# Hybrid RWKV7 and Fox block on one core: group norm split from the chain, inverse transfers on ScalarE's queue, outputs in bursts of four chunks, three gates moved

## The chip, the cores and the metric

The kernel runs on one core of a Trainium2 chip. The metric is the time of one execution on the device in microseconds (us); three runs of the kernel before are shown. The engines are PE (TensorE), DVE (VectorE), ACT (ScalarE), POOL (GpSimd) and SP (SyncE, which here only issues transfers). Each engine works through its own instructions in a fixed order.

## The reference

One block on x of 1024 tokens by 1024 features, float32, one layer:

```python
h = _rmsnorm(x, norm_g)
u_a, u_b, u_g = split(h @ w_in)
y_a = _rwkv7_mixer(u_a, ...) @ w_out_a     # token shift, 8 heads of 64, recurrent state, group norm, silu gate
y_b = _fox_mixer(u_b, ...) @ w_out_b       # 8 heads of 64, causal softmax with forget gates, silu gate
g_a, g_b = split(u_g, 2)
merged = sigmoid(g_a) * y_a + sigmoid(g_b) * y_b
x = x + merged @ w_out
return _rmsnorm(x, final_norm_g)
```

The mixer of RWKV7 is a scan over tokens, state = state*w + (state a) b + v k, y = state r. After it comes a normalisation of each head's 64 values (mean, variance, the norm of groups), then a bonus and the gate.

## The kernel before

Features lie on partitions, tokens on the free axis. x is normed, transposed, and kept as a high and a low part (hTH, hTL); every projection is three passes of matmuls (L311 to L313: high by high, high by low part of x, low part of the weight by high), which PE takes 512 columns at a time. A weight tile is loaded by SP (L218), its high part is cast on ACT (L203), and its low part is subtracted on POOL (L206).

The scan is done in chunks of 64 tokens. There are four **units**, (p, n): p is a group of four heads, n a half of the sequence, in the order (0,0), (0,1), (1,0), (1,1), called units 0 to 3 here. Each has two functions:

- **prep** (from L471): decays, scores within chunks (psc, L565, masked by DVE into QL and Q, L569), then for the 32 triangles of 32 by 32 per head pair an inverse by substitution on DVE. For it the blocks go from QL to a DRAM tile ld by four DMAs (L598), back by one into lt (L602), with one triangle per partition; 30 steps of two DVE operations (L639 etmp, L643) invert them in place; then td (L645, one DMA) and eight DMAs into Tb (L649) bring them back. DVE transposes them into TW (L655), and PE and ACT make the off-diagonal blocks: pw (L661), TW (L663), pz (L669), Tb (L671). Beside the inverse PE makes pk (L628).
- **chain** (from L680): eight chunks in a row, each px (L694), pu (L709), po (L719) on PE with DVE and ACT between, and every four chunks the output matmuls py (L734, 16 per four chunks) and an addition to yv. Behind the eight chunks the same function holds the group norm (L746 to L772): DVE, transposes pt on PE (L761), a gate, and a DMA to yab.

All else before attention is **bulk**, which fills PE while a unit waits: projections of the second group of heads, the 24 gate tiles (ps_gg: 48 matmuls of 512 columns each, in two halves of 24; ACT takes each half out of PSUM at L376, or L334 and DVE for some, and a DMA of ACT's queue stores it as gab<-gt, L359), and the projections of attention (pf, L907 to L909, 24 matmuls of 256 columns each, taken out by ACT as xn<-pf, L910, and squared, L912; pfv, the values). Until attention the bulk has two PSUM banks (tag pj).

Then **attention** for p = 0 to 3 (two heads each): norm_qk transposes the normed q and k (pqk, pqq, L941), writes KA and QA; QA's high part is copied by DMA to the other 64 partitions (L959, L960); attend makes scores (sc, L994), softmax, transposes (pt, L1018) and outputs (L1038, L1039). Beside it run the projections of the next p and the gates that are left. At the end **merge**: pma and pmb (w_out_a, w_out_b, with ya and yb, whose memory is that of hTL and a pool of its own), and the output projection pz.

What sets the order: a scheduler of the framework places the instructions of all engines from their priorities, which follow the program's text, shifted by `order(offset)`. A bulk stretch has an offset of LATER (1000000), a chain one of -LATER. How many gates lie where is written in three tables, by unit (RFILL) and by attention p (FPRE ahead of, FFILL behind the next projection):

```python
RFILL = [5, 6, 6, 2]
FPRE = [1, 1, 2, 0]
FFILL = [1, 3, 2, 0]
```

The first four numbers take 19 gates; the five that are left go to p = 0 (two) and p = 1 (three), and none is left for p = 2 and 3. `tc.issue_after(ins)` makes the instructions inside it stand behind ins.

Of the kernel before, what the change touches and what calls it, by code (L numbers as in the profile page):

```python
# [9 lines left out]
F32 = mybir.dt.float32  # L10
# [61 lines left out]
T1B = 3  # L72
RFILL = [5, 6, 6, 2]
FPRE = [1, 1, 2, 0]
FFILL = [1, 3, 2, 0]

# [14 lines left out]
def kernel(  # L91
# [30 lines left out]
    @contextmanager  # L122
    def order(offset):

        tc.cur_priority += offset
        yield
        tc.cur_priority -= offset
# [350 lines left out]
    def prep(pp_, n):  # L478
# [117 lines left out]
        for e, _, *qs in half:  # L596
            for i, q in enumerate(qs):
                nc.sync.dma_start(  # L598
                    ld[e, i].transpose([1, 0, 2]),
                    QL[q, e].rearrange("p h c t -> p (h c) t")[:, :, HB * i : HB * i + HB],  # L600
                )
        nc.sync.dma_start(lt3, ld.rearrange("e i g s t -> (e i g) s t"))  # L602

# [40 lines left out]
        td = dp.tile([2, 2, NG, HB, HB], F32, tag="td", name=f"td{u}")  # L644
        nc.sync.dma_start(td.rearrange("e i g s t -> (e i g) s t"), lt3)  # L645
        for e, _, *qs in half:
            for i, q in enumerate(qs):
                for h in range(2):
                    nc.sync.dma_start(  # L649
                        Tg[q, h, :, q], td[e, i, UC * h : UC * h + UC].transpose([1, 0, 2])  # L650
                    )
# [26 lines left out]
    def chain(pp_, n, d):  # L678
# [4 lines left out]
        for c in range(UC):  # L683
# [24 lines left out]
            for h in range(2):  # L708
                nc.tensor.matmul(pu[:, h * C : (h + 1) * C], Tb[:, c, h, :], xs[:, h * C : (h + 1) * C], start=True, stop=True)  # L709
            for e, own, other in pairs:  # L710
# [5 lines left out]
            if gc < NCH - 1:  # L716
                po = pp.tile([P, HALF], F32, tag="xus", name=f"po{u}_{c}")
                for e, own, other in pairs:
                    nc.tensor.matmul(po[:, e * P : (e + 1) * P], BKt[:, e, c, :], SV[:, e, c, :], start=True, stop=True)  # L719
                for e, own, other in pairs:  # L720
# [8 lines left out]
            if c % 4 == 3:  # L729
                py = pp.tile([P, HALF], F32, tag="y", name=f"py{u}_{c}").rearrange("p (c h i) -> p c h i", h=2, i=C)  # L730
                for c_ in range(c - 3, c + 1):
                    for h in range(2):
                        for e, own, other in pairs:
                            nc.tensor.matmul(  # L734
                                py[own, c_ % 4, h, :], Q[:, e, h, c_, :], SV[:, e, c_, h * C : (h + 1) * C],
                                start=True, stop=True,
                            )
                yc = yv[:, c - 3 : c + 1]
                nc.vector.tensor_add(yc, yc, py)


        G = 2 * UC
        st = rp.tile([P, 4, G], F32, tag="st", name=f"stat{u}")
# [180 lines left out]
    def norm_qk(p, xn, rr):  # L924
# [10 lines left out]
        for n in range(2):  # L935
            xg = xn[n].rearrange("p b (g i) -> p (b g) i", i=HD)
            (nc.gpsimd if n in NORMPOOL else nc.vector).tensor_mul(xg, xg, rr[n].unsqueeze(2).broadcast_to([P, 16, HD]))
            for c, key in ((1, "k"), (0, "q")):
# [16 lines left out]
                if key == "q":  # L955
                    nc.sync.dma_start(qlo[:, HS[n]], ql.bitcast(F32))
            if n == 1:
                QAf = QA.bitcast(F32)
                nc.sync.dma_start(QAf[B, 0, :], QAf[A, 0, :])  # L959
                nc.sync.dma_start(QAf[A, 1, :], QAf[B, 1, :])  # L960
        return KA, QA, qlo, cb
# [156 lines left out]
    for i, (p, n) in enumerate(units):  # L1118
        d = prep(p, n)
        if i + 1 == len(units):  # L1120
            open_early()
        with bulky():
            if i == 0:
                proj_rkv(2)
                proj_rkv(3)
            fill(RFILL[i], 0)
            if i + 1 == len(units):
                qk = project_qk(0)
                project_v(0)
                forget()  # L1130
        with order(-LATER):
            chain(p, n, d)
    open_late()
# [96 lines left out]
```

## Time and profile before

| | us |
|---|---|
| three runs | 1168.89, 1172.01, 1174.45 (median 1172.01) |
| the profiled execution | 1171.96 |
| its span, first to last instruction | 1170.3 |
| PE busy | 1064.0 (91%) |
| DVE busy | 725.5 (62%) |
| ACT busy | 459.7 (39%) |
| POOL busy | 284.8 (24%) |

The span is cut by the trace into: norm and transposes until about 50 us, first projections until 130, unit 0 until 243, unit 1 until 382, unit 2 until 511, unit 3 until 640, the last group norm until 677, attention from about 692 to 1000, merge until 1076, output projection until the end. Busy times of a PE whose matmuls overlap are modelled; how fast it goes is read from the distance between the starts of two neighbours. The granted clock is 1.00 at 2.4 GHz and 0.50 at 1.2 GHz.

### The profile page before, as it was taken

The numbers are of one execution on the slowest core, as the hardware profiler recorded it, in microseconds if no ns is written. First come the engines' busy times: TensorE is split into PE (matmuls) and PEld (weight loads), VectorE is DVE, ScalarE is ACT, GpSimd is POOL, SyncE is SP. The second block draws the span as 40 slices with busy tenths as digits, with TensorE's granted clock in tenths as the row PEclk, the third lists the DMA queues.
The fourth block names the chain that finished last, engine by engine and source line by source line (L and its number), as shares of the span: only waits on it lengthen the run. The fifth ranks groups of instructions, "written<-read, shape, count | busy, mean of one in ns | idle before, by whom it ended". The sixth has DMA issues, their size and how long they took to land. (4 is left out here: it accounts for less than half of the span.)

```text
span 1170.3 us, 18157 instructions
## 1 busy us (share of the span) xinstructions
PE 1064.0 (91%) x6591; PEld 873.6 (75%) x6591; DVE 725.5 (62%) x1855; ACT 459.7 (39%) x969; POOL 284.8 (24%) x296
## 2 busy tenths in 40 slices
PE   3897998999989898999989979999989788999997
PEld 3676775867768776777888878887968766877886
DVE  7514676588745866386847449686377577466145
ACT  5534232434224331443233346554355355232222
POOL 4420320125110341114201222313222211251400
PEclk9998999999999998999999989999999899999999
DMA  6156434124341343213311151423142150663223
GB/s 207 48 158 211 131 81 114 55 90 123 101 113 46 119 118 108 64 55 83 92 28 38 41 177 42 122 59 91 36 140 86 43 165 19 203 205 114 95 91 126
DMA packets 126043, 118.20 MB, mean 101 GB/s; under 512 B 33361, under 2 KB 91842, under 8 KB 125954
## 3 DMA queue, kind: packets, MB, share of 16 engines
q1 hardware_dynamic: 113664, 94.99, 27.8%
q10 hardware_dynamic: 11714, 21.52, 5.0%
q8 instruction: 52, 0.85, 0.3%
q0 software_dynamic: 576, 0.54, 0.2%
q14 instruction: 37, 0.30, 0.1%
HBM read 79.23 MB, written 35.68 MB: 98 GB/s over the span
## 5 line engine op out<-in xcount | busy, mean ns | idle before, releaser
L311 PE MATMUL ps_gg<-hTH,wH_gg 128*128 128x512 f32 x384 | 158.5, 413 | 3.3 <-DVE gt L338 2.2
L313 PE MATMUL ps_gg<-hTH,wL_gg 128*128 128x512 f32 x384 | 159.4, 415 | 0.0
L312 PE MATMUL ps_gg<-hTL,wH_gg 128*128 128x512 f32 x384 | 157.9, 411 | 0.0
L206 POOL TENSOR_TENSOR wL_gg<-w_gg,wH_gg 128x1024 fp32r<-128x1024 f32 x24 | 60.2, 2508 | 269.6 <-ACT wH_gg L203 263.2
L311 PEld LDWEIGHTS ps_gg<-hTH,wH_gg 128*128 128x128 f32 x384 | 73.4, 191 | 19.3 <-DVE gt L338 3.0
L313 PEld LDWEIGHTS ps_gg<-hTH,wL_gg 128*128 128x128 f32 x384 | 73.9, 192 | 14.6
L312 PEld LDWEIGHTS ps_gg<-hTL,wH_gg 128*128 128x128 f32 x384 | 73.5, 191 | 13.5
L907 PE MATMUL pf<-wqkH,hTH 128*128 128x256 f32 x256 | 74.7, 292 | 0.0
L908 PE MATMUL pf<-wqkL,hTH 128*128 128x256 f32 x256 | 74.7, 292 | 0.0
L909 PE MATMUL pf<-wqkH,hTL 128*128 128x256 f32 x256 | 74.7, 292 | 0.0
L376 ACT ACTIVATE gt<-ps_gg 128x512 f32<-128x512 f32 x40 | 23.9, 598 | 99.9 <-PE ps_gg L313 89.3
L1005 ACT ACTIVATE pr<-pr,mm 128x128 f32<-128x128 f32 (+3 forms) x64 | 49.9, 780 | 28.3 <-DVE mm L1001 27.4
L639 DVE TENSOR_TENSOR etmp<-lt 64x30 f32<-64x30 f32 (+14 forms) x120 | 51.4, 429 | 10.9 <-issue 7.3
L1183 PE MATMUL pz<-wo,mH 128*128 128x512 f32 (+1 forms) x136 | 53.1, 390 | 2.9 <-ACT mH L1092 2.9
L706 ACT ACTIVATE ws<-state,WC 64x64 f32<-64x64 f32 x112 | 38.7, 345 | 40.2 <-DVE state L726 33.5
L1185 PE MATMUL pz<-wo,mL 128*128 128x512 f32 (+1 forms) x136 | 52.6, 387 | 0.0
L1018 PE MATMUL pt<-ident,pr 128*128 128x128 f32 x288 | 48.2, 275 | 4.4 <-DVE pr L1009 4.4
L1184 PE MATMUL pz<-wo,mH 128*128 128x512 f32 (+1 forms) x136 | 52.2, 384 | 0.0
L908 PEld LDWEIGHTS pf<-wqkL,hTH 128*128 128x128 f32 x256 | 49.9, 195 | 0.5
L907 PEld LDWEIGHTS pf<-wqkH,hTH 128*128 128x128 f32 x256 | 49.9, 195 | 0.2
L909 PEld LDWEIGHTS pf<-wqkH,hTL 128*128 128x128 f32 x256 | 49.9, 195 | 0.2
L643 DVE TENSOR_TENSOR lt<-lt,etmp 64x30 f32<-64x30 f32 (+14 forms) x120 | 46.7, 390 | 3.8
(333 smaller groups left out, 2829.5 us busy)
## 6 DMA issues: line engine op xcount, KB each, us to landing
w_gg<-in_w_in_dram SPq DMA_DIRECT2D x24, 512.0 KB, 3.7
gab<-gt ACTq DMA_DIRECT2D x48, 256.0 KB, 2.1
xt<-in_x_dram SPq DMA_DIRECT2D x8, 512.0 KB, 5.8
wqk<-in_w_in_dram SPq DMA_DIRECT2D x16, 256.0 KB, 3.3
cb<-cumd SPq DMA_DIRECT2D x8, 512.0 KB, 5.4
yt<-yab SPq DMA_DIRECT2D x16, 256.0 KB, 3.4
ta<-gab SPq DMA_DIRECT2D x16, 256.0 KB, 3.5
wot<-in_w_out_dram SPq DMA_DIRECT2D x16, 256.0 KB, 2.9
```

The costliest lines, as they stand in the source:

```text
L206: nc.gpsimd.tensor_sub(wL[:, k], w[:, k], wH[:, k])
L311: nc.tensor.matmul(ps, wH[:, k, :], rH[:, k, ts_], start=(k == 0), stop=False)
L312: nc.tensor.matmul(ps, wH[:, k, :], rL[:, k, ts_], start=False, stop=False)
L313: nc.tensor.matmul(ps, wL[:, k, :], rH[:, k, ts_], start=False, stop=(k == nk - 1))
L639: nc.vector.tensor_mul(tm, lt3[:, s, s + 1 :].unsqueeze(1).broadcast_to([4 * NG, s, m]), lt3[:, :s, s].unsqueeze(2).broadcast_to([4 * NG, ...
L907: nc.tensor.matmul(ps, hTH[:, k, bs], wH[:, kk, :], start=(k == 0), stop=False)
L908: nc.tensor.matmul(ps, hTH[:, k, bs], wL[:, kk, :], start=False, stop=False)
L909: nc.tensor.matmul(ps, hTL[:, k, bs], wH[:, kk, :], start=False, stop=(k == KD - 1))
L1005: nc.scalar.activation(pr[:, :w], pr[:, :w], AF.Exp, bias=last, scale=-1.0, accum_out=mm[:, 2:3])
L1183: nc.tensor.matmul(ps, mH[:, k, bs], oH[:, k, c], start=(k == 0), stop=False)
L1184: nc.tensor.matmul(ps, mH[:, k, bs], oL[:, k, c], start=False, stop=False)
L1185: nc.tensor.matmul(ps, mL[:, k, bs], oH[:, k, c], start=False, stop=(k == KD - 1))
```

## The change

It has five parts. RFILL, FPRE and FFILL take 16 gates before attention instead of 19 and leave eight: one for p = 0, two for p = 1, three for p = 2, two for p = 3. The 14 DMAs of each unit's inverse (ld, lt, td, Tb) are issued by ACT instead of SP. The py matmuls stand behind the last po of their four chunks. The group norm is a function of its own, norm_out, with a priority behind the next unit's preparation, save for the last unit. QA's copies are issued for each half of the tokens, as four DMAs of 64 by 512 instead of two of 64 by 1024. All lines behind L716 move down, by one to six (py is L735, pt of the norm L766, xn<-pf L915, sc L998).

```diff
--- before.py
+++ after.py
@@ -70,9 +70,9 @@
 NQEARLY = True
 ATTFIRST = True
 T1B = 3
-RFILL = [5, 6, 6, 2]
-FPRE = [1, 1, 2, 0]
-FFILL = [1, 3, 2, 0]
+RFILL = [4, 5, 5, 2]
+FPRE = [0, 1, 1, 2]
+FFILL = [1, 1, 2, 0]
 
 
 def rsqrt_newton(nc, y, x, t):
@@ -595,11 +595,11 @@
         ld = dp.tile([2, 2, NG, HB, HB], F32, tag="ld", name=f"ld{u}")
         for e, _, *qs in half:
             for i, q in enumerate(qs):
-                nc.sync.dma_start(
+                nc.scalar.dma_start(
                     ld[e, i].transpose([1, 0, 2]),
                     QL[q, e].rearrange("p h c t -> p (h c) t")[:, :, HB * i : HB * i + HB],
                 )
-        nc.sync.dma_start(lt3, ld.rearrange("e i g s t -> (e i g) s t"))
+        nc.scalar.dma_start(lt3, ld.rearrange("e i g s t -> (e i g) s t"))
 
 
         bon = rp.tile([P, UC, 2], F32, tag="bon", name=f"bon{u}")
@@ -642,11 +642,11 @@
             )
             nc.vector.tensor_add(lt3[:, :s, s + 1 :], lt3[:, :s, s + 1 :], tm)
         td = dp.tile([2, 2, NG, HB, HB], F32, tag="td", name=f"td{u}")
-        nc.sync.dma_start(td.rearrange("e i g s t -> (e i g) s t"), lt3)
+        nc.scalar.dma_start(td.rearrange("e i g s t -> (e i g) s t"), lt3)
         for e, _, *qs in half:
             for i, q in enumerate(qs):
                 for h in range(2):
-                    nc.sync.dma_start(
+                    nc.scalar.dma_start(
                         Tg[q, h, :, q], td[e, i, UC * h : UC * h + UC].transpose([1, 0, 2])
                     )
         TW = rp.tile([P, HALF], F32, tag="TW", name=f"TW{u}").rearrange("p (g t) -> p g t", t=HB)
@@ -706,7 +706,7 @@
                             nc.scalar.activation(ws[q, e], st_c[q, e, h, :], AF.Copy, scale=WC[q, e, c : c + 1])
             pu = ps_misc(f"pu{u}_{c}", "late")
             for h in range(2):
-                nc.tensor.matmul(pu[:, h * C : (h + 1) * C], Tb[:, c, h, :], xs[:, h * C : (h + 1) * C], start=True, stop=True)
+                last_mm = nc.tensor.matmul(pu[:, h * C : (h + 1) * C], Tb[:, c, h, :], xs[:, h * C : (h + 1) * C], start=True, stop=True)
             for e, own, other in pairs:
                 nc.vector.tensor_mul(
                     SV[own, e, c].rearrange("p (h i) -> p h i", h=2),
@@ -716,7 +716,7 @@
             if gc < NCH - 1:
                 po = pp.tile([P, HALF], F32, tag="xus", name=f"po{u}_{c}")
                 for e, own, other in pairs:
-                    nc.tensor.matmul(po[:, e * P : (e + 1) * P], BKt[:, e, c, :], SV[:, e, c, :], start=True, stop=True)
+                    last_mm = nc.tensor.matmul(po[:, e * P : (e + 1) * P], BKt[:, e, c, :], SV[:, e, c, :], start=True, stop=True)
                 for e, own, other in pairs:
                     for h, q in ((0, A), (1, B)):
                         o = po[q, e * P + h * C : e * P + (h + 1) * C]
@@ -728,17 +728,22 @@
                             )
             if c % 4 == 3:
                 py = pp.tile([P, HALF], F32, tag="y", name=f"py{u}_{c}").rearrange("p (c h i) -> p c h i", h=2, i=C)
-                for c_ in range(c - 3, c + 1):
-                    for h in range(2):
-                        for e, own, other in pairs:
-                            nc.tensor.matmul(
-                                py[own, c_ % 4, h, :], Q[:, e, h, c_, :], SV[:, e, c_, h * C : (h + 1) * C],
-                                start=True, stop=True,
-                            )
+                with tc.issue_after(last_mm.ins):
+                    for c_ in range(c - 3, c + 1):
+                        for h in range(2):
+                            for e, own, other in pairs:
+                                nc.tensor.matmul(
+                                    py[own, c_ % 4, h, :], Q[:, e, h, c_, :], SV[:, e, c_, h * C : (h + 1) * C],
+                                    start=True, stop=True,
+                                )
                 yc = yv[:, c - 3 : c + 1]
                 nc.vector.tensor_add(yc, yc, py)
 
-
+        return yv
+
+    def norm_out(pp_, n, d, yv):
+
+        u = f"{pp_}_{n}"
         G = 2 * UC
         st = rp.tile([P, 4, G], F32, tag="st", name=f"stat{u}")
         mean, var, rstd, tmp4 = (st[:, j, :] for j in range(4))
@@ -954,10 +959,9 @@
                         )
                 if key == "q":
                     nc.sync.dma_start(qlo[:, HS[n]], ql.bitcast(F32))
-            if n == 1:
-                QAf = QA.bitcast(F32)
-                nc.sync.dma_start(QAf[B, 0, :], QAf[A, 0, :])
-                nc.sync.dma_start(QAf[A, 1, :], QAf[B, 1, :])
+            QAf = QA.bitcast(F32)[:, :, HS[n]]
+            nc.sync.dma_start(QAf[B, 0], QAf[A, 0])
+            nc.sync.dma_start(QAf[A, 1], QAf[B, 1])
         return KA, QA, qlo, cb
 
     sc_tags = SCTAGS
@@ -1129,7 +1133,9 @@
                 project_v(0)
                 forget()
         with order(-LATER):
-            chain(p, n, d)
+            yv = chain(p, n, d)
+        with order(LATER // 2 if i + 1 < len(units) else -LATER):
+            norm_out(p, n, d, yv)
     open_late()
     bulk_tags[:] = FTAGS
     qk = norm_qk(0, *qk)
```

ACT, unit 3, from the last gate ahead of the inverse's end to TW. Before:

```order
L376 ACTIVATE gt10_1_5145<-ps_gg10_1_5120 128x512 [waits DMAHW2_49,PE_49]
L203 CAST wvH0_0_5424<-wv0_0_5426 128x1056 [waits DMAHW1_49,DMAHW0_49,Pool_49]
L359 DMA gab_316<-gt10_1_5145 128x512 [waits Activation_49]
L910 COPY xn0_0_5162<-pf0_0_0_5164 128x256 [waits PE_49]
L912 ACTIVATE sq0_0_0_5190<-pf0_0_0_5164 128x256
L910 COPY xn0_0_5162<-pf0_0_1_5193 128x256 [waits PE_49]
L912 ACTIVATE sq0_0_1_5219<-pf0_0_1_5193 128x256
L910 COPY xn0_0_5162<-pf0_0_2_5222 128x256 [waits PE_49]
L912 ACTIVATE sq0_0_2_5248<-pf0_0_2_5222 128x256 [waits DVE_49]
L663 COPY TW1_1_4945<-pw1_1_4950 32x512 [waits PE_49]
L663 COPY TW1_1_4945<-pw1_1_4950 32x512
L910 COPY xn0_0_5162<-pf0_0_3_5251 128x256 [waits PE_49]
```

Changed:

```order
L203 CAST wvH0_0_5238<-wv0_0_5240 128x1056
L645 DMA td1_1_4749<-lt1_1_4586 64x1024 [waits DMAHW1_49,DVE_49]
L649 DMA Tb_421<-td1_1_4749 32x8x32 [waits DMAHW5_49]
L649 DMA Tb_421<-td1_1_4749 32x8x32 x3
L649 DMA Tb_421<-td1_1_4749 32x8x32 [waits DMAHW2_49]
L649 DMA Tb_421<-td1_1_4749 32x8x32 [waits DMAHW3_49]
L649 DMA Tb_421<-td1_1_4749 32x8x32 [waits DMAHW4_49]
L649 DMA Tb_421<-td1_1_4749 32x8x32
L915 COPY xn0_0_4976<-pf0_0_0_4978 128x256 [waits PE_49]
L917 ACTIVATE sq0_0_0_5004<-pf0_0_0_4978 128x256
L915 COPY xn0_0_4976<-pf0_0_1_5007 128x256 [waits PE_49]
L917 ACTIVATE sq0_0_1_5033<-pf0_0_1_5007 128x256
```

td (L645, which waits for DVE's last operation on lt) and the eight Tb DMAs (the first of which waits for td to land) now stand ahead of the copies xn<-pf, which free the two PSUM banks; before they were SP's.

PE, unit 3, around the first pw, before:

```order
L909 MATMUL pf0_0_2_5222<-wqkH0_0_5148,hTL_73 128x256
L907 MATMUL pf0_0_2_5222<-wqkH0_1_5155,hTH_72 128x256
L661 MATMUL pw1_1_4950<-TW1_1_4945,Tb_421 32x32 [waits DVE_49,PE_49]
L908 MATMUL pf0_0_2_5222<-wqkL0_1_5156,hTH_72 128x256
L909 MATMUL pf0_0_2_5222<-wqkH0_1_5155,hTL_73 128x256
L907 MATMUL pf0_0_2_5222<-wqkH0_1_5155,hTH_72 128x256
```

Changed:

```order
L914 MATMUL pf0_0_1_5007<-wqkH0_1_4969,hTL_73 128x256
L661 MATMUL pw1_1_4764<-TW1_1_4759,Tb_421 32x32 [waits DVE_49,PE_49,Pool_49]
L661 MATMUL pw1_1_4764<-TW1_1_4759,Tb_421 32x32 [waits DVE_49,Pool_49]
L661 MATMUL pw1_1_4764<-TW1_1_4759,Tb_421 32x32 x15
L661 MATMUL pw1_1_4764<-TW1_1_4759,Tb_421 32x32 [waits DVE_49,Pool_49]
L661 MATMUL pw1_1_4764<-TW1_1_4759,Tb_421 32x32 x14
L912 MATMUL pf0_0_2_5036<-wqkH0_0_4962,hTH_72 128x256 [waits Activation_49]
```

Before, the bulk behind pk and ahead of the first pw is one and a half gates (ps_gg9_0 to ps_gg10_1), pf0_0_0, pf0_0_1 and a half of pf0_0_2; now it is the rest of pf0_0_0 and all of pf0_0_1. From the last psc to the first pw of unit 3 the order has 107 matmuls of gates and 61 of pf before, 13 and 48 now, and from there to the first pu 50 and 20 of pf. In unit 1 it is 177 of gates before and 142 now, then 28 and 14. In units 0 and 2 these numbers change by five or fewer.

PE, unit 1's chain, an output group and its neighbours, before:

```order
L312 MATMUL ps_gg22_0_2938<-hTL_73,wH_gg22_2932 128x512
L313 MATMUL ps_gg22_0_2938<-hTH_72,wL_gg22_2933 128x512
L719 MATMUL po0_1_0_3265<-SV0_1_2456,BKt0_1_2455 128x128 [waits DVE_49] x2
L734 MATMUL py0_1_3_3347<-SV0_1_2456,Q0_1_2453 64x64 x4
L311 MATMUL ps_gg22_0_2938<-hTH_72,wH_gg22_2932 128x512
L312 MATMUL ps_gg22_0_2938<-hTL_73,wH_gg22_2932 128x512
L694 MATMUL px0_1_1_3273<-state1_424,AR0_1_2452 128x128 [waits DVE_49]
```

Changed:

```order
L312 MATMUL ps_gg22_0_2938<-hTL_73,wH_gg22_2932 128x512
L313 MATMUL ps_gg22_0_2938<-hTH_72,wL_gg22_2933 128x512 [waits Pool_49]
L719 MATMUL po0_1_3_3216<-SV0_1_2392,BKt0_1_2391 128x128 [waits DVE_49] x2
L735 MATMUL py0_1_3_3223<-SV0_1_2392,Q0_1_2389 64x64 x16
L694 MATMUL px0_1_4_3242<-state0_423,AR0_1_2388 128x128 [waits DVE_49,PE_49,Activation_49]
L694 MATMUL px0_1_4_3242<-state0_423,AR0_1_2388 128x128 [waits DVE_49]
L311 MATMUL ps_gg22_0_2938<-hTH_72,wH_gg22_2932 128x512
```

py stood in groups of four, one behind each chunk's po, and stands now in one burst of 16 behind the fourth chunk's po. Over the program 32 groups become eight bursts.

PE at the first scores of attention p = 0, before:

```order
L908 MATMUL pf1_1_0_6781<-wqkL1_0_6636,hTH_72 128x256
L909 MATMUL pf1_1_0_6781<-wqkH1_0_6635,hTL_73 128x256
L907 MATMUL pf1_1_0_6781<-wqkH1_0_6635,hTH_72 128x256
L994 MATMUL sc0_0_0_0_0_6043<-KA0_5983,QA0_5984 128x256 [waits DMAHW1_49,PE_49]
L994 MATMUL sc0_0_0_1_0_6053<-KA0_5983,QA0_5984 128x256 [waits PE_49]
L908 MATMUL pf1_1_0_6781<-wqkL1_0_6636,hTH_72 128x256
```

Changed:

```order
L912 MATMUL pf1_1_2_6593<-wqkH1_1_6396,hTH_72 128x256
L913 MATMUL pf1_1_2_6593<-wqkL1_1_6397,hTH_72 128x256
L914 MATMUL pf1_1_2_6593<-wqkH1_1_6396,hTL_73 128x256
L998 MATMUL sc0_0_0_0_0_5859<-KA0_5797,QA0_5798 128x256 [waits DMAHW3_49,PE_49,Activation_49]
L998 MATMUL sc0_0_0_1_0_5869<-KA0_5797,QA0_5798 128x256 [waits PE_49]
L912 MATMUL pf1_1_3_6622<-wqkH1_0_6389,hTH_72 128x256 [waits Activation_49]
```

The first two sc stand now one block of pf earlier, and read only the first half of QA.

For the group norm, in units 1 and 2 its transposes pt (L761, now L766) stand where they stood: on PE ahead of the next unit's pss and psc, on DVE its operations ahead of the masks of L569. Ahead of pt there are ten more matmuls of gates in the first case and four more in the second.

## Rows read from the trace of the kernel before

**Rows 1.** Part 1 of the page: busy us, share, instructions.

```profile
PE 1064.0 (91%) x6591; PEld 873.6 (75%) x6591; DVE 725.5 (62%) x1855; ACT 459.7 (39%) x969; POOL 284.8 (24%) x296
```

**Rows 2.** Busy time by stage: elapsed, then each engine's busy us (instructions), granted clock, DMA share, GB/s.

```profile
690.70:697.50 6.80, 5.25 (x24) 5.10 (x25) 0.73 (x4) 0.47 (x2) 0.29 (x1) 0.50 0.43 124
740.00:808.00 68.00, 67.36 (x481) 59.80 (x480) 49.86 (x147) 39.53 (x100) 14.79 (x33) 1.00 0.25 75
925.00:1000.00 75.00, 61.24 (x325) 47.09 (x324) 57.95 (x150) 39.29 (x88) 14.19 (x24) 0.93 0.30 95
929.60:939.80 10.20, 7.84 (x22) 5.96 (x23) 7.39 (x12) 2.50 (x5) 2.64 (x1) 0.50 0.51 164
```

**Rows 3.** PE's waits: line, releaser, us in total, times, longest.

```profile
PE pw L661 <- DVE TW L655: 14.9, 4, 4.2
...
PE sc L994 <- DMA QA<-QA: 7.0, 2, 6.2
PE pt L761 <- DVE yv L756: 5.3, 3, 3.1
...
PE pma L312 <- DVE ya L1054: 4.1, 3, 1.8
PE pma L311 <- ACT ya L1053: 3.0, 1, 3.0
```

**Rows 4.** Timeline of PE in unit 3: start, us, operation, idle before it.

```profile
544.73 2.05 PE L565 MATMUL psc<-AR,BK 64*128 64x128 f32 x16
...
588.40 0.28 PE L661 MATMUL pw<-TW,Tb 32*32 32x32 f32 x2 [3.80 <-DVE TW L655]
...
593.23 0.69 PE L661 MATMUL pw<-TW,Tb 32*32 32x32 f32 x32
...
599.41 0.66 PE L709 MATMUL pu<-xs,Tb 128*128 128x64 f32 x4
```

**Rows 5.** Timeline of DVE in unit 3: first and last operation of the inverse.

```profile
554.75 0.18 DVE L639 TENSOR_TENSOR etmp<-lt 64x30 f32<-64x30 f32 x1
...
582.41 0.21 DVE L643 TENSOR_TENSOR lt<-lt,etmp 64x30 f32<-64x30 f32 x1
```

**Rows 6.** Timeline of ACT in unit 3.

```profile
580.28 0.37 ACT L910 COPY xn<-pf 128x256 f32<-128x256 f32 x1 [1.28 <-PE pf L909]
```

**Rows 7.** Part 5 of the page: busy us, mean ns, idle before.

```profile
L639 DVE TENSOR_TENSOR etmp<-lt 64x30 f32<-64x30 f32 (+14 forms) x120 | 51.4, 429 | 10.9 <-issue 7.3
...
L643 DVE TENSOR_TENSOR lt<-lt,etmp 64x30 f32<-64x30 f32 (+14 forms) x120 | 46.7, 390 | 3.8
```

**Rows 8.** SP's issues in unit 1, from the first ld to lt.

```profile
281.28 0.32 SPq L598 DMA_DIRECT2D ld<-QL  x1
284.47 0.32 SPq L772 DMA_DIRECT2D yab<-yo  x1
...
290.12 0.56 SPq L602 DMA_DIRECT2D lt<-ld  x1
```

**Rows 9.** Timeline of DVE in unit 1, ahead of the inverse.

```profile
297.43 0.75 DVE L338 SCALAR_TENSOR_TENSOR gt<-ps_gg,col,t_gg 128x511 f32<-128x511 f32 x1 [4.84 <-DMA gab<-gt]
```

**Rows 10.** Timeline of PE in unit 1: py and its neighbour behind it.

```profile
353.70 0.45 PE L734 MATMUL py<-SV,Q 128*64 128x64 f32 x8
354.09 0.50 PE L313 MATMUL ps_gg<-hTH,wL_gg 128*128 128x512 f32 x1
```

**Rows 11.** Timeline of PE at attention's first scores.

```profile
685.69 0.28 PE L909 MATMUL pf<-wqkH,hTL 128*128 128x256 f32 x1
685.81 0.28 PE L907 MATMUL pf<-wqkH,hTH 128*128 128x256 f32 x1
692.25 0.77 PE L994 MATMUL sc<-KA,QA 128*128 128x256 f32 x2 [6.16 <-DMA QA<-QA]
```

**Rows 12.** Timeline of PE in the merge: two neighbours of 512 columns.

```profile
941.19 0.40 PE L311 MATMUL pma<-ya,wH_oa 128*128 128x512 f32 x1
941.42 0.39 PE L312 MATMUL pma<-ya,wH_oa 128*128 128x512 f32 x1
```

## The prediction

> **What bounds the kernel now.** The page first: PE is busy for 1064 of 1170.3 us, far ahead of the others [rows 1]. So the time is PE's work plus what PE loses, and a change counts if it shortens PE's work, or takes away or makes a wait or a stretch at the low clock. Then the table of stages: where attention has bulk beside it PE is busy for 67.4 of 68 us, but between 925 and 1000 us, when the gates have run out, for only 61.2 of 75 [rows 2]; in the same table the granted clock is 0.50 in two of the stretches behind a wait. Then PE's waits: first stands pw, the end of the inverse, once in each unit, then the scores' wait for QA's copy, the group norm's transposes and the merge's wait for ya [rows 3]. Last the timelines of unit 3, to see how long the inverse is and what covers it.
>
> A matmul of a gate takes 0.23 us of PE (941.19 to 941.42 [rows 12]), one of pf 0.12 (685.69 to 685.81 [rows 11]).
>
> **Unit 3, the largest term.** The last psc ends at 546.78 and the first pu starts at 599.41 [rows 4]: 52.6 us, set by a row of dependent steps. Of these 8.0 us lie ahead of the inverse (to 554.75), the inverse takes 27.9 (to 582.62 [rows 5]), and 16.8 follow. PE hardly notices now, since the bulk lasts almost as long: pw waits for 3.80 us. The change takes away that cover. By the order its 107 matmuls of gates fall to 13, and its 61 + 50 of pf (ahead of the first pw, and from there to pu) to 48 + 20: 94 x 0.23 + 43 x 0.12 = 27 us less work in this window. It can't be filled from behind: pf0_0_2 needs a PSUM bank, ACT frees it only after td and the eight Tb DMAs, and td waits for DVE's last operation on lt. Before, the same copy ran at 580.28, ahead of that end [rows 6]. The steps get somewhat shorter: 30 pairs at the mean of 429 and 390 ns are 24.6 us [rows 7] instead of 27.9, because no weight is split on POOL at that time and no gate's work stands between, and a little may go behind the inverse; I take 4 us. So PE loses 27 - 4 = **+23 us**. Bounds: +15 if the steps shrink by 12, +28 if they don't shrink and a low clock follows.
>
> **Unit 1.** There 177 + 28 matmuls of gates become 142 + 14, 49 x 0.23 = 11.3 us less cover. Against it: SP's first ld goes out at 281.28 and lt only at 290.12, with the norm's yab and loads between [rows 8]; that is 8.8 us, of which I think 4 to 5 are SP's order, and ACT has none of those transfers in its queue. A gate operation of DVE, which stands ahead of the inverse, was idle for 4.84 us before 297.43 [rows 9]; with less PE work ahead of it about 2.5 go. I take 11.3 - 7.3 = **+4**; bounds 0 (everything is returned) and +11 (nothing).
>
> The Trainium skill (DMA: Bandwidth & Descriptors, Issuing engines are not separate DMA queues) states that transfers of all issuing engines run on the same 16 DMA engines, and that another issuer saves only the issue time. By that rule alone unit 1's term would be +11, and the sum 1182.5 us; the trace of before can't show it, since there all of these go out on SP. The rows speak for a middle: what lt waits for there is SP's order, and not bandwidth [rows 8].
>
> **Units 0 and 2.** Cover and inverse stay. New is that ACT stands at td while gates' copies queue behind it; the tiles ahead of pw fit the two banks, so I take **+1**; bounds -1 (SP free for weights) and +4 (one bank missed in each).
>
> **py in bursts.** A group of four stretches from 353.70 to 354.09, 0.39 us [rows 10]; 16 make 1.56 in four groups. The nearest row for a burst of 32 records is pw, 0.69 [rows 4]. (1.56 - 0.69) x 8 = -7; since the last py now comes later for the norm, **-6.5**; bounds -4 and -8.
>
> **Gates at p = 2 and 3.** From 925 to 1000 us PE is idle for 13.8 us [rows 2]. The merge's waits for ya in it, 4.1 + 3.0 = 7.1 [rows 3], stay: ya lies where hTL was, and the last gate reads that, so they come behind the last gate instead. The rest should go as at 740 to 808 us, where gates lie beside attention: **-7**. Bounds: -14 if the merge's waits go too, -3 if two more gates per p make DVE and ACT late. Moving a gate costs PE nothing by itself: 48 matmuls here or there.
>
> **QA's halves.** The first scores wait for 6.16 us [rows 11], and behind that the clock is at 0.50 for 6.8 us, in which 24 matmuls take twice their time, some 2.5 us [rows 2]. Now these scores need the first half only, which is copied a block earlier. 6.2 + 2.5 = -8.7, less the next wait (QZ, and the second pair of scores behind 24 pf): **-7**; bounds -3 and -9. Four issues instead of two on SP lie beside other work; if not, they cost under 2 us in all.
>
> **The group norm.** Its split moves almost nothing: in units 1 and 2 pt stands ahead of pss and psc as before. Ten and four more gate matmuls ahead of it, 2.3 and 0.9 us, go against waits of 5.3 in three [rows 3], with a low clock behind two of them. The last norm has 31 us of bulk ahead. **-4**; bounds 0 and -7.
>
> **The sum** is made against the profiled execution, 1171.96 us, which lies 0.05 under the median of the runs: 23 + 4 + 1 - 6.5 - 7 - 7 - 4 = +3.5, so **1175.5 us**. A measurement of this kernel tells about 0.5% from no change, here 5.9 us: 1166.1 to 1177.9 counts as the same.
>
> **The rivals.**
> 1. Slower, by ACT's queue. ACT waits for DVE at td in every unit, and everything behind it, copies out of PSUM and the chain's ws among them, starts late. It decides from the point at which PE needs a third bank before lt is done. Unit 3 shows that in the order; in the others the tiles just fit, so if the inverse is two or three us late there as well, PE stands. With units 0 and 2 at +4, unit 1 at +11 and unit 3 at +25 the sum is +15.5: **1187.5 us**. For it: pw is already the first of PE's waits [rows 3]. Against: SP was held by other work in unit 1.
> 2. Faster, the hole is small and attention gives all. If unit 3 loses 15, unit 1 gains back most of its cover (+2), units 0 and 2 cost nothing, and py -7, attention -12, QA -8.5 and norm -5 come in, the sum is -15.5: **1156.5 us**. For it: 13.8 us of idle PE at the end of attention are there to take. Against: the 27 us of removed cover come from the order, and nothing in the rows makes the inverse 12 us shorter.
> 3. The norm's part does nothing, as its order suggests: 4 less, **1179.5 us**; and the queue's change returns nothing to unit 1: 1182.5 us.
>
> **How the numbers follow.** The forecast and what lies near it, 1166 to 1178: 0.38. Slower: 0.35, of which 0.2 for rival 1 and 0.15 for rival 3. Faster: 0.27, rival 2 and smaller sums of its kind. Half the widths of the bounds, 6.5, 5.5, 2.5, 2, 5.5, 3 and 3.5, come to 11.7 as independent errors; the steps whose latencies I can't see widen that to some 16: 1158 to 1191, which takes in rival 1 and nearly rival 2.
>
> **What would show it.** In the profile after, pw of unit 3 should wait for about 25 us, with PE empty between pf0_0_1 and the inverse's end and ACT at td; pw of unit 1 for 7 or more. py should appear as eight bursts of about 0.7 us. The wait of sc for QA should be under 2 us, and PE between the last pqq and the last attention output busy as at 740 to 808 us, with the ya waits behind the last gate. The prediction is wrong if unit 3's pw waits for under 12 us, if its inverse is far from 25 us, or if attention with gates still leaves more than 8 us idle in p = 3.

## The result, and the profile after

| | before | after |
|---|---|---|
| median of four runs each, us | 1172.96 | 1190.05 |
| lowest to highest | 1168.89 to 1174.45 | 1189.0 to 1190.68 |
| span of the profiled execution | 1170.3 | 1188.2 |

The ratio is 1.015, with an interval of 1.0123 to 1.0178: the change makes the kernel slower, by about 17 us. That lies at the upper end of the range (1158 to 1191), 14.5 above the time predicted.

Part 1 of the page after, as [rows 1]:

```profile
PE 1060.2 (89%) x6591; PEld 875.6 (74%) x6591; DVE 733.6 (62%) x1855; ACT 458.3 (39%) x969; POOL 282.9 (24%) x296
```

PE's work is no larger (1060.2 against 1064.0 us), the span is 17.9 longer. So no work was added, and the loss is waits and what a low clock adds. PE's waits after, as [rows 3] (line, releaser, us in total, times, longest):

```profile
PE pw L661 <- DVE TW L655: 39.0, 6, 24.4
PE ps_r L311 <- DVE last_k L344: 14.1, 3, 5.6
...
PE ps_gg L311 <- DVE gt L338: 8.6, 2, 7.7
PE pt L766 <- DVE yv L761: 7.2, 3, 4.5
...
PE sc L998 <- DMA QA<-QA: 4.0, 1, 4.0
...
PE pma L311 <- ACT ya L1057: 0.5, 1, 0.5
```

Two rows of the same view before, which the prediction did not use:

```profile
PE ps_r L311 <- DVE last_k L344: 8.6, 2, 5.2
...
PE ps_gg L311 <- DVE gt L338: 2.2, 2, 1.4
```

pw, in all units together, waits for 24.1 us more than before (14.9), which was expected. ps_r and ps_gg together wait for 11.9 us more, which was not. pt waits for 1.9 more. sc waits for 3.0 less, and the 7.1 us for ya have almost gone.

**Unit 3.** The timelines of PE, DVE and ACT there (start, us, operation, idle before it), as [rows 4 to 6]:

```profile
561.65 0.28 PE L914 MATMUL pf<-wqkH,hTL 128*128 128x256 f32 x1
586.33 0.28 PE L661 MATMUL pw<-TW,Tb 32*32 32x32 f32 x2 [24.40 <-DVE TW L655]
...
597.40 0.95 PE L709 MATMUL pu<-xs,Tb 128*128 128x64 f32 x4
```

```profile
557.51 0.18 DVE L639 TENSOR_TENSOR etmp<-lt 64x30 f32<-64x30 f32 x1
...
580.94 0.20 DVE L643 TENSOR_TENSOR lt<-lt,etmp 64x30 f32<-64x30 f32 x1
```

```profile
558.24 1.08 ACT L203 CAST wvH<-wv 128x1056 fp32r<-128x1056 f32 x1
581.17 0.46 ACTq L645 DMA_DIRECT2D td<-lt  x1
584.08 3.82 ACTq L649 DMA_DIRECT2D Tb<-td  x8
587.94 0.37 ACT L915 COPY xn<-pf 128x256 f32<-128x256 f32 x1 [28.62 <-DMA Tb<-td]
```

PE ends its last pf and stands for 24.40 us, until the inverse is through and its blocks are back. The inverse takes 23.6 us (557.51 to 581.14) instead of 27.9. ACT stands from its cast to the xn copy. How much work the window from the end of the last psc to the first pu holds is read from its busy time, after and then before (elapsed, busy us and instructions of PE, PEld, DVE, ACT, POOL, granted clock, DMA share, GB/s):

```profile
548.05:597.40 49.35, 23.09 (x297) 20.90 (x298) 28.34 (x76) 10.18 (x20) 4.42 (x5) 0.66 0.16 36
```

```profile
546.78:599.41 52.63, 48.83 (x434) 41.73 (x435) 34.58 (x87) 15.86 (x30) 9.22 (x7) 0.97 0.28 74
```

PE has 137 matmuls and 25.7 us of busy time less in it, but the window is only 3.3 us shorter. The granted clock averages 0.66 over it, against 0.97.

**Attention.** Stretches in the same place, around the start of p = 3, before [rows 2] (925 to 1000) and after:

```profile
901.00:982.00 81.00, 78.23 (x488) 66.46 (x487) 53.67 (x154) 42.01 (x96) 17.88 (x26) 0.98 0.25 75
```

PE is idle for 2.8 of 81 us, where it was for 13.8 of 75.

**Units 0 to 2.** The same window, from the end of the last psc to the first pu, takes 60.6 us in unit 0 before and after, and 56.3 and 57.2 in unit 2. In unit 1 it takes 67.5 before and 64.2 after; but before, 205 matmuls of gates lay in it, and after 156.

### The profile page after: what moved, and what is told of

Same layout as the page of the kernel before. It is cut to its first block, busy times and chain, and to the rows that moved or that the text cites. A ratio compares the mean times of both kernels' runs of the same rounds, so it can differ in the third digit from the quotient of the medians.

```text
span 1188.2 us, 18172 instructions
## 1 busy us (share of the span) xinstructions
PE 1060.2 (89%) x6591; PEld 875.6 (74%) x6591; DVE 733.6 (62%) x1855; ACT 458.3 (39%) x969; POOL 282.9 (24%) x296
## 5 line engine op out<-in xcount | busy, mean ns | idle before, releaser
L311 PE MATMUL ps_gg<-hTH,wH_gg 128*128 128x512 f32 x384 | 161.7, 421 | 8.8 <-DVE gt L338 8.6
L313 PEld LDWEIGHTS ps_gg<-hTH,wL_gg 128*128 128x128 f32 x384 | 75.0, 195 | 13.2
L1042 PE MATMUL po<-PH,V 128*128 128x256 f32 x160 | 46.3, 303 | 1.7 <-ACT PH L1027 1.1
```

The lines of the kernel that those rows point to most:

```text
L311: nc.tensor.matmul(ps, wH[:, k, :], rH[:, k, ts_], start=(k == 0), stop=False)
L313: nc.tensor.matmul(ps, wL[:, k, :], rH[:, k, ts_], start=False, stop=(k == nk - 1))
```

## The experiments

Each kernel was timed against the kernel before on the same chip. Where the edit says "alone", all else is the kernel before. The ratio is taken over all runs and need not be the quotient of the two medians. Traces show one execution each.

| run | edit | median, us | before, us | ratio (interval) |
|---|---|---|---|---|
| e1_tables | tables alone | 1183.55 | 1168.93 | 1.0124 (1.0084 to 1.0164) |
| e2_act_queue | 14 transfers on ACT alone | 1187.51 | 1168.93 | 1.0141 (1.0095 to 1.0188) |
| e3_py_bursts | py bursts alone | 1160.66 | 1168.93 | 0.9918 (0.9885 to 0.995) |
| e4_qa_halves | QA halves alone | 1173.96 | 1168.93 | 1.0041 (1.002 to 1.0062) |
| e5_norm | norm split alone | 1168.99 | 1171.22 | 0.9984 (0.9965 to 1.0002) |
| e6_ld_lt_on_act | ld and lt alone | 1178.25 | 1171.22 | 1.0054 (1.0034 to 1.0074) |
| e7_td_tb_on_act | td and Tb alone | 1167.98 | 1171.22 | 0.9959 (0.994 to 0.9978) |
| e8_qa_halves_cb_behind | QA halves, cb behind them | 1178.44 | 1171.22 | 1.0049 (1.0022 to 1.0077) |
| e9_change_old_tables | the change, old tables | 1189.05 | 1169.89 | 1.0175 (1.0142 to 1.0208) |
| e10_py_norm_td_tb | py, norm, td and Tb | 1161.7 | 1169.89 | 0.9943 (0.9918 to 0.9969) |
| e11_gates_respread | e10 and gates spread anew | 1148.57 | 1169.89 | 0.9823 (0.9793 to 0.9852) |
| e12_change_sp_queue | the change, SP's queue | 1174.16 | 1171.5 | 1.0025 (1.0002 to 1.0049) |

### What makes the hole in unit 3: the tables or the queue

e1 takes the three tables alone:

```diff
-RFILL = [5, 6, 6, 2]
-FPRE = [1, 1, 2, 0]
-FFILL = [1, 3, 2, 0]
+RFILL = [4, 5, 5, 2]
+FPRE = [0, 1, 1, 2]
+FFILL = [1, 1, 2, 0]
```

> The kernel before with the three tables of the change alone; transfers, py, norm and QA stay. By its order unit 3 has 6.7 us of bulk from the last psc to the first pu (38.0 before, 11.1 in the change), the other units as before. Cover theory (the moved gates were what PE did beside the last inverse): pw of unit 3 waits for 25 to 30 us though ACT holds no transfer, attention gives back 7 to 12, and the run is 12 to 20 us slower than before, 1185 to 1193. Queue theory (ACT standing at td is what costs): pw of unit 3 stays under 10 us, and the run is 0 to 10 us faster than before.

e2 takes the queue alone: `nc.sync` becomes `nc.scalar` at ld, lt, td and Tb (L598, L602, L645, L649).

> The kernel before with the 14 transfers of each inverse on ScalarE's queue alone; tables, py, norm and QA stay. Unit 3 keeps 39.1 us of bulk beside its inverse; unit 1 has 36.1 instead of 47.8. Cover theory: unit 3's pw waits for under 8 us, the run is 0 to 8 us slower than before. Queue theory: ACT's copies stand behind td in every unit, pw waits rise in all four, and the run is 12 us or more slower.

PE at the first pw of unit 3 in e1:

```profile
584.81 0.28 PE L661 MATMUL pw<-TW,Tb 32*32 32x32 f32 x2 [23.34 <-DVE TW L655]
```

With the tables alone, and td and Tb on SP, the hole is there in full; with the queue alone pw's longest wait is 6.4 us. So the hole comes from the cover that the tables take away, and ACT's standing at td makes at most the 1 us by which it is longer in the change. PE stands because pw is the next instruction in its own order. Yet the tables cost 14.6 us net, less than their hole, because attention gives time back: around the start of p = 3 (906.9 to 981.9) PE is idle for 3.1 of 75 us in e1. In unit 1 the tables take no cover away: 205 matmuls of gates lie there in e1, as before, and 155 in e2. So what unit 1 loses comes with the queue. The queue alone costs as much, and by something else, as the next runs show.

### What in the queue costs

e6 and e7 split it: ld and lt on ACT, td and Tb on SP, and the reverse.

```diff
-        nc.sync.dma_start(lt3, ld.rearrange("e i g s t -> (e i g) s t"))
+        nc.scalar.dma_start(lt3, ld.rearrange("e i g s t -> (e i g) s t"))
```

> The kernel before with ld and lt on ScalarE's queue, td and Tb still on SP. If lt on ACT, behind copies that wait for PE, is what costs, with DVE's evictions queued behind an inverse that starts late, most of the 16 us of the whole queue's move show here: 8 to 16 us slower, with ps_r and ps_gg waiting for DVE (L344, L338) about 5 us each in units 0 and 1. If ACT standing at td costs, the run is within 4 us of before.

```diff
-        nc.sync.dma_start(td.rearrange("e i g s t -> (e i g) s t"), lt3)
+        nc.scalar.dma_start(td.rearrange("e i g s t -> (e i g) s t"), lt3)
```

> The kernel before with td and Tb on ScalarE's queue, ld and lt still on SP. If ACT standing at td until DVE is done is what costs, 8 to 16 us slower, with the pw waits longer by 2 to 3 in each unit. If lt on ACT costs, within 4 us of before.

ld and lt cost 0.5%; td and Tb, by which rival 1 argued, make the kernel 0.4% faster. One of ACT's waits in e7 behind Tb:

```profile
ACT xn L910 <- DMA Tb<-td: 7.0, 1, 7.0
```

With two more, of 6.9 us (gt) and 6.8 us (t_k), ACT stands for some 7 us at the same place in three of the units, and the kernel is none the slower for it. What lt costs is seen in unit 0. ACT before, then after:

```profile
147.37 0.59 ACT L578 COPY BKt<-pb 128x512 f32<-128x512 f32 x1 [0.26 <-PE pb L577]
147.85 0.69 ACT L334 ACTIVATE t_k<-ps_k,col 128x512 f32<-128x512 f32 x1
```

```profile
154.06 0.51 ACTq L602 DMA_DIRECT2D lt<-ld  x1
...
155.72 0.59 ACT L632 COPY AK<-pk 128x512 f32<-128x512 f32 x1 [0.52 <-PE pk L628]
...
156.82 0.68 ACT L334 ACTIVATE t_k<-ps_k,col 128x512 f32<-128x512 f32 x1
```

DVE and PE after:

```profile
160.56 0.14 DVE L639 TENSOR_TENSOR etmp<-lt 64x30 f32<-64x30 f32 x1 [3.99 <-issue]
...
160.95 2.33 DVE L639 TENSOR_TENSOR etmp<-lt 64x58 f32<-64x58 f32 x1
163.20 0.73 DVE L338 SCALAR_TENSOR_TENSOR kx<-ps_k,col,t_k 128x511 f32<-128x511 f32 x1
...
164.27 0.14 DVE L344 COPY last_k<-ps_k 128x1 f32<-128x1 f32 x1
```

```profile
158.51 0.49 PE L313 MATMUL ps_k<-hTH,wL_k 128*128 128x512 f32 x1
164.56 0.76 PE L311 MATMUL ps_r<-hTH,wH_r 128*128 128x512 f32 x1 [5.56 <-DVE last_k L344]
```

This is the chain of causes. ACT's first copy t_k of a projection out of PSUM stood between two BKt copies. It now stands behind lt and the copies of SV and AK, which wait for PE, and comes 9 us later, though PE had ended that half of the projection at 148.5. DVE's half of the same eviction (L338, L344), which before was done at 152.19, therefore comes behind the start of the inverse, which waits for lt. So no bank is free, and ps_r stands for 5.56 us. Some 2 us of them are the one long step at 160.95, which starts 0.09 us behind a subtraction on POOL (160.86, 2.34 us); the last section shows what such steps are.

In e6 unit 0 is longer with such a wait: from the end of the last psc to the first pu it takes 65.6 us there, 60.6 before and 56.5 in e7. In the change, with both halves on ACT, it is 60.6 again.

In unit 1 it is the gate's eviction, and PE waits for 7.65 us:

```profile
301.19 0.80 PE L311 MATMUL ps_gg<-hTH,wH_gg 128*128 128x512 f32 x1 [7.65 <-DVE gt L338]
```

DVE in unit 1 after:

```profile
293.46 0.18 DVE L639 TENSOR_TENSOR etmp<-lt 64x30 f32<-64x30 f32 x1
...
300.38 0.75 DVE L338 SCALAR_TENSOR_TENSOR gt<-ps_gg,col,t_gg 128x511 f32<-128x511 f32 x1
```

Here ACT's half of the eviction was not late (282.80). But DVE's half stood ahead of the inverse before [rows 9], and now stands behind its first six pairs of steps. The inverse gains by it: it starts 13.7 us behind the start of the last psc group, where it was 20.3. It then takes 33.9 us instead of 30.1.

In e6 the two waits are there as well (ps_r 13.2, ps_gg 9.1 in total); in e7 they are as before (8.3 and 2.2). The halves do not add up: +0.5% and -0.4% alone, +1.4% together. In e2 pw waits for 17.0 (e6 14.0) and a value projection pfv for 6.3 us (e6 1.8); which of the scheduler's choices brings these about stays open.

### py, QA and the norm, one by one

e3 puts the 16 py behind the last po of their four chunks, as in the change, and nothing else.

> The kernel before with the py matmuls in bursts of 16 alone. Prediction's price: 6.5 us faster (4 to 8), eight bursts of about 0.7 us instead of 32 groups that take 0.39. Rival: the time between is idle anyway, or the later py makes the norm late, and the run is within 2 us of before.

It is 0.8% faster. A burst in the changed kernel and what follows it on PE (the trace has two records for each of the 16 matmuls):

```profile
223.13 1.15 PE L735 MATMUL py<-SV,Q 128*64 128x64 f32 x32
224.21 0.90 PE L694 MATMUL px<-state,AR 128*128 128x128 f32 x4
```

A burst takes 1.08 us (223.13 to 224.21), not the 0.69 that was taken from pw. Against 1.56 in four groups that is 3.8 us over eight bursts; the rest of the gain has to lie elsewhere, and pt's wait, 2.8 instead of 5.3 us in e3, is one part that shows. A part is the stretch from the first pu of unit 1 to the end of unit 2's last psc: 71.8 us before, 68.3 in e3. With the queue it is lost again: that stretch takes 72.8 us in the change and 73.1 in e9, but 67.4 in e12, with the same bursts. In the change pt waits there for 4.5 us, in e12 for 0.6; what makes it wait stays open.

e4 takes QA's four copies alone:

```diff
-            if n == 1:
-                QAf = QA.bitcast(F32)
-                nc.sync.dma_start(QAf[B, 0, :], QAf[A, 0, :])
-                nc.sync.dma_start(QAf[A, 1, :], QAf[B, 1, :])
+            QAf = QA.bitcast(F32)[:, :, HS[n]]
+            nc.sync.dma_start(QAf[B, 0], QAf[A, 0])
+            nc.sync.dma_start(QAf[A, 1], QAf[B, 1])
```

> The kernel before with QA's copies by halves alone; the order of PE up to attention is that of before. Prediction's price: 7 us faster (3 to 9), the wait of the first sc for QA under 2 us and no low clock behind it. Rival: the wait goes over to the next scores or to QZ, and the run is within 2 us of before.

The wait does not move: 6.24 us. SP and PE in e4:

```profile
681.37 0.38 SPq L821 DMA_DIRECT2D wv<-in_w_in_dram  x1
...
682.36 1.72 SPq L934 DMA_DIRECT2D cb<-cumd  x2
684.43 0.48 SPq L958 DMA_DIRECT2D QA<-QA  x1
...
686.15 0.47 SPq L959 DMA_DIRECT2D QA<-QA  x1
```

```profile
683.23 0.60 PE L941 MATMUL pqq<-ident,xn 128*128 128x128 f32 x4
...
691.84 0.77 PE L993 MATMUL sc<-KA,QA 128*128 128x256 f32 x2 [6.24 <-DMA QA<-QA]
```

PE's last pqq ahead of the scores, before:

```profile
681.34 0.60 PE L941 MATMUL pqq<-ident,xn 128*128 128x128 f32 x4
```

The trace of e4 is 1.9 us late by then, so the two are compared from this pqq on. The first half goes out 1.2 us behind it, where the whole copy went out 2.2 us behind (683.52), and the scores start 8.6 us behind it, where it was 10.9 [rows 11]. So the halves do land 2.3 us sooner. But the scheduler moves the scores forward as well: PE has 15 matmuls of pf between that pqq and the scores, where it had 35. It gets to the scores 2.3 us sooner, and waits as long.

The copies are still slow. The first half stands behind a weight and cb in SP's order, its second copy is issued at 686.15, and the scores start 5.7 us later, while the DMA engines are busy:

```profile
684.40:691.80 7.40, 1.20 (x11) 0.99 (x9) 2.61 (x4) 1.49 (x4) 0.00 (x0) 0.75 0.86 254
```

e8 adds to e4 that the two cb transfers stand behind QA's copies (`tc.issue_after(qa_last.ins)`).

> QA's copies by halves, and the two broadcasts of cb, 512 KB each, issued behind the four copies instead of ahead of them. If the halves did nothing because their packets queue behind cb's, the first sc's wait for QA falls from 6.2 to under 2.5 us and the run is 3 to 7 us faster than the halves alone. If the copies themselves take that long, the wait stays at 5 us or more.

By the wait and the time that theory fell: 5.5 us at the first scores, and +0.5%. By the copies it did not: the scores start 6.4 us behind the last pqq, where it was 8.6 in e4. They have moved forward once more, with two matmuls of pf ahead of them, and PE waits almost as long. Where e4 and e8 lose their 0.4 and 0.5% isn't shown.

What does shorten this wait is the tables: at the first scores 1.5 us in e1 and 2.9 in e11, both with whole copies, and in e1 no weight is issued near QA's copy. With halves and the new tables the scores start 5.4 us behind the last pqq in the change and 4.9 in e12, with the old tables 8.1 in e9. That the weight's traffic is what delays QA was not tried by itself.

e5 takes the split of the norm alone.

> The kernel before with the group norm as a function of its own and with the change's priority, alone. The prediction: pt stays ahead of the next unit's psc, so at most 4 us faster, waits of pt for yv 2 to 5 in place of 5.3; bulk beside the inverses as before but for 2.8 us less in unit 1. Rival: the priority brings other work ahead, and the run is 5 us or more slower or faster.

Its interval takes in no change.

### The tables within the change, and what would be faster

e9 is the change with the tables of before.

> The whole change with the three tables of the kernel before, so 19 gates again before attention. Unit 3 has 39.6 us of bulk beside its inverse. Cover theory: its pw waits for under 8 us and the run is 10 to 18 us faster than the change, 1172 to 1180. If the parts overlap (single prices add to 24 where the whole change cost 17), what the tables cost in this company is less than their 14.6 alone: 5 to 10.

Beside the other four parts the tables cost nothing net: 1.0175 without them, 1.015 with them. The hole of 24 us is gone in e9 (pw's longest wait is 6.8), but PE waits for pfv for 6.6 us, for QA for 6.0 and for ya for 5.7.

e10 keeps what paid or cost nothing alone: py, the norm and td with Tb on ACT.

> The three parts that gained or cost nothing alone, together: py in bursts, the group norm apart, td and Tb (not ld and lt) on ScalarE's queue; tables and QA as before. Sum of the single prices: 9.6 + 1.9 + 4.8 = 16 us faster than before, 1155. If they gain the same waits twice, 8 to 12.

It is 0.6% faster, not the 16 us of the sum, and no faster than py alone (0.8%). So gains don't add here either.

e11 adds to e10 another spread of the five gates in attention, one, one, one and two, with all 19 gates ahead of it kept:

```diff
-FPRE = [1, 1, 2, 0]
-FFILL = [1, 3, 2, 0]
+FPRE = [0, 0, 1, 2]
+FFILL = [1, 1, 0, 0]
```

> As the run with py, norm, td and Tb, with the five gates left for attention spread as one, one, one and two over p = 0 to 3 instead of two and three over the first two; no gate leaves the units, so the inverses keep their cover. Prediction's term for attention by itself: 3 to 7 us faster than that run, with less idle PE in p = 3. Rival: p = 0 and 1 lose what p = 3 gains, and it is within 2 us.

It is 1.8% faster than the kernel before, and 13 us faster than e10, where 3 to 7 were expected. A stretch of e11 around the start of p = 3:

```profile
896.00:972.00 76.00, 71.33 (x408) 57.35 (x407) 58.15 (x151) 43.79 (x94) 19.14 (x26) 1.00 0.38 122
```

PE is idle for 4.7 of 76 us, as against 13.8 of 75 [rows 2], and pw's longest wait is 4.2. What the change wanted from attention is to be had without taking cover from unit 3.

e12 is the change with SP's queue.

> The whole change with the 14 transfers of the inverse on SP's queue again; tables, bursts, halves and norm as changed. It asks what the queue costs inside the change, where alone it costs 16. Theory (the parts do not add: what the queue costs by late evictions in units 0 and 1 and what the tables cost by the hole in unit 3 lie in different places, so the hole stays and the rest comes back): pw of unit 3 still waits for 22 to 25 us, ps_r and ps_gg behind DVE wait for under 12 us together (22.7 in the change), and the time is that of the other four parts one by one, 14.6 - 9.6 + 4.8 - 1.9 = +8 on the kernel before, 1174 to 1182 us, some 11 less than the change. Rival 1 (the queue costs nothing once fewer gates lie ahead of attention, since its loss is only moved into the hole): 1187 to 1193, as the change. Rival 2 (ACT at td makes the hole): pw of unit 3 waits for under 12 us and the time is under 1168.

PE's waits in e12:

```profile
PE pw L661 <- DVE TW L655: 36.5, 4, 23.4
...
PE ps_r L311 <- DVE last_k L344: 8.3, 2, 5.1
...
PE ps_gg L311 <- DVE gt L338: 0.8, 1, 0.8
```

The hole stays, the two waits of the queue are gone, and the time is 1174.16, at the lower end of the first theory. So within the change the queue costs about 1.25% (1.015 less 1.0025), some 15 us, and alone 1.4% (e2). The tables cost 1.24% alone and nothing net beside the other four parts (e9). Why they cost less there is not shown: no run has py, QA's halves and the norm without tables and queue.

## Why the prediction was right or wrong

**Right: unit 3.** PE's busy time in it fell by 25.7 us where 27 were forecast, and the window got 3.3 us shorter; that is a loss of 22.4 where 23 were forecast. The inverse shrank by 4.3 us where 4 were, and pw's longest wait is 24.4 us, where about 25 were to be seen. e1 and e12 tie it to the tables. Wrong there was one step: that the hole "can't be filled from behind" because ACT frees a bank only after td. It is as long in e1 and e12, where ACT does not issue td; in e12 ACT waits for PE then, for 27.9 us, in place of the reverse.

**Right: units 0 and 2.** "Cover and inverse stay", with +1, came out as 0.0 and +0.9 us in the windows. In unit 0 a loss by lt (+5.0 in e6) meets a gain by td and Tb (-4.1 in e7); neither was forecast.

**A size off: unit 1.** +4 was forecast: 11.3 us of cover less 7.3 given back. By the order 49 matmuls of gates (11.3 us) did go, but only 3.3 us came back, so the term was about +8. "ACT has none of those transfers in its queue" held as far as it went: lt goes out 8.9 us behind the start of the last psc group instead of 12.2, and the inverse starts 6.7 us sooner. The step that failed is that this is then given back whole: the inverse takes 3.8 us longer, and PE stands 7.65 us for a bank. The 4.84 us of idle time which the prediction put to PE's work is put down to a DMA (gab<-gt) in its row [rows 9].

**Put at nothing: what the queue does elsewhere.** The prediction counted the queue in the four windows only: 11.3 - 7.3 + 1 = +5, against some 15 within the change and 16.5 alone. In the change the stretch between units 1 and 2 is 5.4 us longer than in e12, which undoes py's gain there. For ld and lt the prediction looked only at what ACT has ahead of them. It didn't look at what they have behind them: t_k moved from ahead of the last BKt copy to behind lt, and DVE's half of the eviction came behind the first steps of the inverse. Rival 1 had the right sign and a time 2.6 us from the measured one, but not the mechanism: it charged td and Tb, which cost nothing (e7), and not ld and lt (e6).

**Wrong: QA's halves.** The step was "these scores need the first half only, which is copied a block earlier". The copy does land earlier, by 2.3 us in e4. But the scores stand earlier too, so the work that covered the copy went with it, and the wait in e4 is 6.24 us where under 2 was forecast. -7 was forecast and +0.4% measured; the wait falls in the change (7.0 to 4.0 us) with the tables, not with the halves.

**A size off: attention.** The merge's ya waits, which were to "stay" behind the last gate, went away: 7.1 us before, 0.5 + 0.3 after. PE's idle time around p = 3 fell by 11.0 us (13.8 to 2.8) where -7 was forecast; the bound of -14 had been meant for that case.

**A size off: py.** -6.5 was forecast, 0.8% measured, some 9.6 us (interval 5.8 to 13.4), but the burst itself gives only 3.8 of them. In the change most of it doesn't show, since the stretch between units 1 and 2 lost it again.

**Near: the norm.** -4 with bounds of 0 and -7; e5 has 0.16% and takes in zero.

The forecast said no change, and 17 us were lost. Each part alone, against its own terms: the queue 16.5 us where +5, QA 4.8 where -7, the tables 14.6 where 23 - 7 = 16, py -9.6 where -6.5, the norm -1.9 where -4. The single prices add up to 24, and the whole change costs 17, so they overlap. That the time lies inside the range, 1 us from its end, is in part luck: the misses of the queue and of QA alone come to 23 us, and py and the overlap kept the time below 1191. (Half the widths of the bounds come to 11.6, not 11.7.)

**Issuing queues.** e6 and e7 move transfers from one issuing engine to another, and the time goes up in one and down in the other. The Trainium skill (DMA: Bandwidth & Descriptors, Issuing engines are not separate DMA queues) states that another issuer saves only the issue time. The runs agree as far as bandwidth goes: the page of the profile has 101 GB/s on average before and 99 after, and from issue to landing ld takes 1.7 us and Tb 2.0 us (medians) on either issuer, lt 5.0 on SP and 4.0 on ACT. They show beyond it that a transfer's place among its issuer's other instructions can cost more than it saves.

## What to carry to other kernels

When DMAs move to an engine that also computes, read the new order for what now stands behind them there, and on the engine that consumes them, and ask which banks those instructions free; here that mattered more than what stands ahead of the DMAs. When a transfer is made shorter, check whether its consumer has moved forward with it: the wait is what the transfer takes less the work that the order still puts before it. Work moved out of a stretch to fill another should come from places with cover to spare: here the same idle time in attention was filled by spreading five gates anew, without touching the 27 us that covered the inverse. Price the parts one by one before putting them together, and then together, since their prices do not add: one that paid, one with no clear effect and three that cost stood here in one change.

## What the runs showed of the hardware

The 4 us by which the inverse was to shrink have a cause that the rows show more sharply than expected. DVE's long steps in unit 3 before, and what POOL ran then:

```profile
555.68 2.33 DVE L639 TENSOR_TENSOR etmp<-lt 64x84 f32<-64x84 f32 x1
...
567.99 2.52 DVE L643 TENSOR_TENSOR lt<-lt,etmp 64x240 f32<-64x240 f32 x1
...
579.21 2.43 DVE L643 TENSOR_TENSOR lt<-lt,etmp 64x84 f32<-64x84 f32 x1
```

```profile
555.50 2.41 POOL L206 TENSOR_TENSOR wqkL<-wqk,wqkH 128x1024 fp32r<-128x1024 f32 x1 [6.18 <-ACT wqkH L203]
567.85 2.40 POOL L206 TENSOR_TENSOR wqkL<-wqk,wqkH 128x1024 fp32r<-128x1024 f32 x1 [9.94 <-ACT wqkH L203]
579.08 2.47 POOL L206 TENSOR_TENSOR wvL<-wv,wvH 128x1056 fp32r<-128x1056 f32 x1 [8.83 <-ACT wvH L203]
```

A DVE operation that starts 0.13 to 0.18 us behind such a subtraction on POOL lasts until that ends: 2.33 and 2.43 us for a step of 64x84, which takes 0.24 elsewhere in the same trace. After, one POOL subtraction lies in unit 3's inverse instead of three. Two steps that are 2.1 us shorter each make 4.2 of the 4.3 us that the inverse lost in length.

The Trainium skill (SBUF — State Buffer, Who interferes with whom) states that a VectorE instruction with two SBUF inputs contends with a GpSimd instruction that reads SBUF, and that the port pair which the two share is an exclusive lock. Both kinds of row above have two SBUF inputs, and the trace agrees: the later one ends with the earlier one.

ACT as an issuer is the second point. It stands for 7 us at Tb in three units of e7, which is no slower for it, and for 28.62 us in unit 3 of the changed kernel, where the hole is at most 1 us longer than in e1, without that. What ACT does late counted here where a bank or another engine hung on it.
